# Prompt attention by pairs of heads: scores at two row places, a mask made by the scan, fp32 weights and values at two column places

## The chip, the cores and the metric

One NeuronCore of a Trainium2 chip runs the whole program in one launch. The metric is the device time in microseconds; the median of three runs stands for a kernel. The engines are named as in the profile: PE (TensorE), PEld (its weight loads), DVE (VectorE), ACT (ScalarE), POOL (GpSimd) and SP, whose queue issues all DMAs here.

## The reference

One step of a hybrid encoder layer, for a prompt of 1024 frames and for 8 decode sequences of 16 new frames with 1024 past ones. Width 1024, 16 heads of 64: group A (8 heads) has stick-breaking attention, group B (8 heads) has softmax attention over the own chunk of 64 frames and the 8 before it, with a learned bias.

```python
def stick_breaking(q, k, v, q_pos, k_pos):
    z = jnp.einsum('bqhd,bkhd->bhqk', q, k).astype(jnp.float32) * (HEAD_DIM ** -0.5)
    causal = k_pos[None, :] < q_pos[:, None]
    log_keep = jnp.where(causal, jax.nn.log_sigmoid(-z), 0.0)
    between = lax.cumsum(log_keep, axis=3, reverse=True) - log_keep
    w = jnp.where(causal, jnp.exp(jax.nn.log_sigmoid(z) + between), 0.0)
    return jnp.einsum('bhqk,bkhd->bqhd', w.astype(v.dtype), v)

def trunk_layer(x, p, ...):
    h = rmsnorm(x, g_mix)
    q_a, k_a, v_a, q_b, k_b, v_b = split_heads(h, w_in)
    a, o_b = stick_breaking(...), chunk_band_prompt(q_b, k_b, v_b, rel_table)
    mix = concat(rmsnorm(a), rmsnorm(o_b))           # per head
    x = x + mix @ w_out
    h = rmsnorm(x, g_ffn)
    x = x + (jax.nn.silu(h @ w_gate) * (h @ w_up)) @ w_down
    return x + sigmoid(rmsnorm(x, g_ple) @ w_ple_gate) * (p @ w_ple_proj)
```

All inputs and outputs are fp32.

## The kernel before

Most products are taken in three fp32r matmuls: both operands are split into a high part (rounded to fp32r) and a low part (the rest), and high x high, high x low and low x high are summed in PSUM (`mm3`, lines 105 to 108). The stages follow each other in this order and overlap at their borders.

1. *Projection* (`qkv`). Transposed, normed inputs stand in SBUF; weights come in column blocks of 256. It is a generator with 96 steps, each the matmuls of one output tile (24 of 256 or 384 columns). Queries and keys are written to DRAM transposed and split (`qkT`), values split in halves side by side (`vhl`).
2. *Decode of group A* beside the projection, up to some 333 us.
3. *Prompt attention* (`attention`). It is a generator too. A unit is one head and one tile `t` of 128 queries; there are 8 pairs of heads (the first 4 of group A), 16 heads, 128 units. One step of `run` does the scores of unit i, the flip of unit i-5 (`LAG`), the outputs of unit i-7 where `t` is odd, and the turn and finish of a head or pair that is through.
   - `head` loads, for one head, queries high and low on the two halves of the partitions, and the keys' high parts twice and low parts twice, so that two matmuls over 128 rows give all four partial products (lines 583 and 584). For group A a third matmul in bf16 adds -1e30 over the diagonal block (line 586). Scores have two PSUM banks (`s=2`).
   - Group A: ACT makes w = sigmoid(s) and keep = sigmoid(-s), DVE scans keep from the right (line 597), POOL multiplies w by the scanned keep (line 598). Group B: DVE adds the bias and takes the maximum (line 592), ACT takes the exponential (line 600).
   - `flip` transposes w by blocks of 128 x 128 on PE (line 616), four to a bank; ACT copies the bank rounded to fp32r into `wth` (line 620), DVE writes the rest into `wtl` (line 111, `sub`).
   - `outputs` multiplies values by weights, for two query tiles (256 columns) at once: the stationary operand holds the 64 high and the 64 low value columns of one head, so that two matmuls, with `wth` and `wtl`, make the sum's two halves on the two halves of the partitions (lines 639 and 640); ACT copies it out (line 643).
   - `turn` transposes the result back (line 654), DVE adds the halves (line 655); `finish` norms it and writes it to `mixp`.
   Transposes, outputs and turns share four PSUM banks (`t=4`), also with the transposes of the second decode (line 403) and of the embedding (line 842).
4. Beside attention run, one after the other: the last 30 projection steps, the *decode of group B* with the embedding product, and the mix with half of the output product. `advance(main, side, ratio)` interleaves two generators in program order. A planner orders each engine's instructions by its own costs, except where `manual_schedule` names engines: those keep the order of the program.
5. The other half of the output product, the feed-forward in seven products of blocks instead of eight (lines 1064 and 1327), the gate and the last norm.

## Time and profile before

| | |
|---|---|
| median of 3 runs | 1720.27 us (1717.31 to 1722.22) |
| span of the profiled execution | 1715.2 us; its own device time isn't listed, so it is read against the runs |
| busy share | PE 97%, PEld 83%, DVE 62%, ACT 47%, POOL 47% |
| chain that ended last | PE 81%, DVE 5%, DMA 5%, ACT 4% |
| moved by DMA | 293.48 MB |
| first score matmul, last flip | 333.4 us, 792.2 us |

The span runs from the first to the last instruction of the profiled execution; the time around it (start and end of the launch) is in the runs' times only. A row of the groups reads: line, engine, operation, output <- inputs by the program's names, shapes, count, then the busy time of the group in us and the mean duration of one in ns, then the idle time of the engine just before them and what ended it. Rows of the timeline begin with start and duration in us. Busy time counts a matmul to the end of its way through the array, so neighbouring matmuls overlap in it.

### The profile page before, as it was taken

How to read it: one execution, taken by the hardware profiler on the slowest of the kernel's cores; microseconds unless marked ns; L12 is line 12 of the kernel's file. 1: busy time of each engine (PE TensorE's matmuls, PEld its weight loads, DVE VectorE, ACT ScalarE, POOL GpSimd, SP SyncE). 2: the span in 40 equal slices, each digit the busy share in tenths (PEclk: the TensorE clock that was granted, in tenths of full speed). 3: DMA queues.
4: the chain of work that ended last, by engine and by line, in shares of the span. 5: the costliest groups of instructions: out<-in, count | busy, mean ns of one | idle time of the engine just before them, and what ended most of it. 6: DMA issues, size and time to landing. Idle time of an engine off the chain costs nothing.

```text
span 1715.2 us, 27832 instructions
## 1 busy us (share of the span) xinstructions
PE 1656.5 (97%) x10404; PEld 1421.2 (83%) x10404; DVE 1071.8 (62%) x1646; ACT 809.9 (47%) x1713; POOL 809.9 (47%) x590
## 2 busy tenths in 40 slices
PE   8999999999997999898989999999999999999998
PEld 7998888989996787787868888888888878888887
DVE  6111444367788766754787666655666587798875
ACT  5223545366677777643553333333333254433673
POOL 2313311277356512322355555555555379957763
PEclk9999999999999999999999999999999999999999
DMA  5846888666469895955423222222222597722222
GB/s 192 277 148 217 275 287 292 188 187 172 120 174 273 256 290 156 256 176 171 148 66 116 95 96 88 86 87 93 95 94 89 204 387 255 259 72 108 102 99 98
DMA packets 172808, 293.48 MB, mean 171 GB/s; under 512 B 16641, under 2 KB 96257, under 8 KB 170370
## 3 DMA queue, kind: packets, MB, share of 16 engines
q1 hardware_dynamic: 172674, 291.71, 52.0%
q8 instruction: 82, 1.34, 0.3%
q14 instruction: 52, 0.43, 0.1%
HBM read 204.77 MB, written 86.90 MB: 170 GB/s over the span
## 4 chain that ended last, share of the span: by engine, by line
PE 81%; DVE 5%; DMA 5%; ACT 4%; issue 2%; POOL 2%; SPq 0%; POOLq 0%; ACTq 0%; DVEq 0%
PE ps L1064 24%; PE ps L106 7%; PE ps L107 7%; PE ps L108 7%; PE pt L1327 4%; PE pt L1064 3%; PE ps L1327 3%; PE pt L616 3%; PE pt L403 3%; PE po L640 2%; PE po L639 2%; PE S L583 2%; PE acc L471 2%; PE sdec L426 1%; DMA v<-sv 1%
## 5 line engine op out<-in xcount | busy, mean ns | idle before, releaser
L111 POOL TENSOR_TENSOR wlo<-wraw,whi 128x512 fp32r<-128x512 f32 (+1 forms) x119 | 212.4, 1809 | 139.6 <-ACT whi L155 139.6
L106 PE MATMUL ps<-whi,hTh 128*128 128x256 f32 x576 | 168.5, 293 | 1.6 <-ACT st L263 1.6
L107 PE MATMUL ps<-wlo,hTh 128*128 128x256 f32 x576 | 165.2, 287 | 0.0
L108 PE MATMUL ps<-whi,hTl 128*128 128x256 f32 x576 | 164.9, 286 | 0.0
L597 DVE TENSOR_TENSOR_SCAN keep<-keep,zero 128x128 f32<-128x128 f32 (+4 forms) x64 | 102.1, 1604 | 32.6 <-ACT keep L589 32.2
L155 ACT CAST whi<-wraw 128x512 fp32r<-128x512 f32 (+1 forms) x122 | 88.6, 744 | 71.5 <-PE ps L1064 28.2
L598 POOL TENSOR_TENSOR w<-w,keep 128x127 f32<-128x127 f32 (+4 forms) x64 | 83.0, 1306 | 79.4 <-DVE keep L597 54.4
L106 PEld LDWEIGHTS ps<-whi,hTh 128*128 128x128 f32 x576 | 111.2, 193 | 7.5 <-issue 5.4
L107 PEld LDWEIGHTS ps<-wlo,hTh 128*128 128x128 f32 x576 | 111.3, 193 | 0.1
L108 PEld LDWEIGHTS ps<-whi,hTl 128*128 128x128 f32 x576 | 111.0, 193 | 0.5 <-DVE hTl L111 0.2
L111 DVE TENSOR_TENSOR wtl<-pt,wth 128x512 fp32r<-128x512 f32 (+1 forms) x192 | 94.4, 514 | 25.4 <-ACT wth L620 24.7
L620 ACT CAST wth<-pt 128x512 fp32r<-128x512 f32 (+1 forms) x192 | 85.1, 467 | 40.6 <-PE pt L616 40.1
L616 PE MATMUL pt<-ident,w 128*128 128x128 f32 x528 | 88.7, 280 | 6.6 <-DVE wtl L111 2.9
L639 PE MATMUL po<-wth,vk 128*128 128x256 f32 (+1 forms) x304 | 76.6, 283 | 0.4 <-DVE osb L655 0.4
L616 PEld LDWEIGHTS pt<-ident,w 128*128 128x128 f32 x528 | 62.3, 142 | 17.5 <-issue 5.0
L111 POOL TENSOR_TENSOR actl<-actr,acth 128x1024 fp32r<-128x1024 f32 (+1 forms) x22 | 61.5, 2795 | 32.4 <-DMA sr<-acts 20.7
L583 PE MATMUL S<-qk 128*128 128x384 f32 (+2 forms) x192 | 71.7, 375 | 5.0 <-ACT keep L589 3.1
L640 PE MATMUL po<-wtl,vk 128*128 128x256 f32 (+1 forms) x304 | 73.0, 283 | 0.0
L404 DVE COPY kT<-pt 128x512 f32<-128x512 f32 x48 | 33.0, 688 | 52.8 <-PE pt L403 48.8
L106 PE MATMUL ps<-hTh,whi 128*128 128x384 f32 x192 | 65.8, 343 | 0.0
L107 PE MATMUL ps<-hTl,whi 128*128 128x384 f32 x192 | 65.6, 342 | 0.0
L108 PE MATMUL ps<-hTh,wlo 128*128 128x384 f32 x192 | 65.2, 339 | 0.0
(446 smaller groups left out, 5276.9 us busy)
## 6 DMA issues: line engine op xcount, KB each, us to landing
draw<-in_cache_sb_k SPq DMA_DIRECT2D x32, 512.0 KB, 6.0
draw<-in_cache_sb_v SPq DMA_DIRECT2D x32, 512.0 KB, 6.0
act<-sg SPq DMA_DIRECT2D x11, 1152.0 KB
actr<-act SPq DMA_DIRECT2D x22, 576.0 KB, 5.4
wraw<-in_w_in SPq DMA_DIRECT2D x11, 1024.0 KB
wraw<-in_w_gate SPq DMA_DIRECT2D x11, 1024.0 KB, 5.6
wraw<-in_w_up SPq DMA_DIRECT2D x11, 1024.0 KB
v<-sv SPq DMA_DIRECT2D x36, 256.0 KB, 4.2
```

The costliest lines, as they stand in the source:

```text
L106: T.matmul(out, lhsT=ah, rhs=bh, start=start, stop=False)
L107: T.matmul(out, lhsT=ah, rhs=bl, start=False, stop=False)
L108: T.matmul(out, lhsT=al, rhs=bh, start=False, stop=stop)
L111: return eng.tensor_tensor(out, a, hi.bitcast(F32), op=ALU.subtract)
L155: A.copy(h[:, o], v[:, o])
L583: T.matmul(sc, lhsT=hd["qq"][:, qs], rhs=hd["kkh"][:, kc], start=True, stop=False)
L597: V.tensor_tensor_scan(rev, rev, zero[:, 0:1].to_broadcast([P, n]), 1.0, op0=ALU.mult, op1=ALU.add)
L616: T.transpose(pt[:, (c - c0) * P : (c - c0 + 1) * P], w[:, c * P : (c + 1) * P], ident)
L639: T.matmul(dst, lhsT=vs, rhs=wth[:, kb - base, c0:c1], start=(i == 0), stop=False)
L640: T.matmul(dst, lhsT=vs, rhs=wtl[:, kb - base, c0:c1], start=False, stop=(i == nkb - 1))
L1064: T.matmul(out, lhsT=a[x][:, k], rhs=b[y][:, k], start=(not more and k == 0 and n == 0), stop=(k == 3 and n == 2), skip_group_check=more)
L1327: T.matmul(out, lhsT=a[i][:, x, m * P : (m + 1) * P], rhs=b[j][:, x], start=(not more and x == 0 and n == 0), stop=(x == 1 and n == 2), sk ...
```

## The change

- A unit is a pair of heads and a query tile: 64 units. `LAG` is 2 units instead of 5; per step, the outputs of unit i-3 come first, then the scores of unit i, then the flip of unit i-2. The ratios of `advance` are halved or doubled accordingly. In the stretch beside the projection PE keeps the order of the program.
- Scores: three matmuls (high x high, high x low, low x high) for each of the two heads, on rows 0 to 63 and 64 to 127, alternately, into a bank for each head. Queries and keys are loaded once for the pair, in two halves of 512.
- The mask matmul goes. Group A's scan runs twice: over the diagonal block with the identity as second operand (`max`), which sets the running product to one at the diagonal and leaves zero beyond it, and then over the rest. A memset clears the last column of w.
- The weights are copied out of PSUM once, unsplit in fp32, by DVE and ACT in turn. Values are stored and loaded unsplit. `outputs` takes one fp32 matmul per head and key block, the two heads at columns 0 to 63 and 64 to 127.
- The result needs no addition of halves; it is turned back once for the pair.
- PSUM: `s=4, t=2`. Scores of group B are cut 256 columns from the end; the bias is loaded in two parts.

```diff
-LAG, RAWS, PT = 5, 7, 2
+LAG, RAWS, PT = 2, 7, 2
...
-    maskb = cst.tile([P, P], BF16, name="maskb")
...
-    vhl = [dram.tile([2, NT * P, 512], F32, name=f"v{g}") for g in range(2)]
+    vd = [dram.tile([2, NT * P, 256], F32, name=f"v{g}") for g in range(2)]
...
-                    for o in range(3):
-                        sv = stg.tile([P, 2, 384], F32R, name="sv", tag="sq").rearrange("p a b -> p (a b)")[:, :512]
-                        sv = sv.rearrange("p (h x d) -> p h x d", h=4, x=2)
-                        flat = st[:, o].rearrange("p (h d) -> p h d", d=HD)
-                        A.copy(sv[:, :, 0, :], flat)
-                        sub(G, sv[:, :, 1, :], flat, sv[:, :, 0, :])
-                        tok = slice((g * 3 + o) * P, (g * 3 + o + 1) * P)
-                        nc.sync.dma_start(vhl[grp][c, tok, :], sv.bitcast(F32).rearrange("p h x d -> p (h x d)"))
+                    rows = slice(g * 384, (g + 1) * 384)
+                    nc.sync.dma_start(vd[grp][c, rows, :].rearrange("(t p) n -> p t n", p=P), st)
...
+        def keys(pr, half):
+
+            grp, p_ = divmod(pr, 4)
+            cs = slice(half * 512, half * 512 + 512)
+            k = ap_.tile([P, 2, 512], F32R, name="k", tag=f"k{half}", bufs=2 - half)
+            for x in range(2):
+                nc.sync.dma_start(k[:, x].bitcast(F32), qkT[grp][1][x][p_][:, cs])
+            st[pr]["k", half] = k
+
+        def queries(pr, half):
+            grp, p_ = divmod(pr, 4)
+            cs = slice(half * 512, half * 512 + 512)
+            q = ap_.tile([P, 2, 512], F32R, name="q", tag=f"q{half}", bufs=1)
+            for x in range(2):
+                nc.sync.dma_start(q[:, x].bitcast(F32), qkT[grp][0][x][p_][:, cs])
+            st[pr]["q", half] = q
+
+        def values(pr, half):
+            grp, p_ = divmod(pr, 4)
+            v = ap_.tile([P, 4, P], F32, name="v", tag=f"v{half}", bufs=2 - half)
+            src = vd[grp][p_ // 2, half * 512 : half * 512 + 512, p_ % 2 * P : p_ % 2 * P + P]
+            nc.sync.dma_start(v, src.rearrange("(t p) n -> p t n", p=P))
+            st[pr]["v", half] = v
...
+            width = (7, 8, 6)[t % 3] * P
+            ws = [ap_.tile([P, width], F32, name="w", tag=f"w{t % 3}{hh}")[:, :n] for hh in range(2)]
+            keep = []
             if not grp:
+                for hh in range(2):
+                    turn[0] = (turn[0] + 1) % 3
+                    keep.append(ap_.tile([P, D], F32, name="keep", tag=f"keep{turn[0]}")[:, :n])
...
+            q = s_["q", t // 4][:, :, t % 4 * P : t % 4 * P + P]
+            lo = 0
+            while lo < n:
+                if grp:
+                    hi = n - 256 if n > 256 and lo == 0 else n
+                else:
+                    hi = n if lo else min(n, 512)
+                sc = [ps["s"].tile([P, 512], F32, name="S", tag="S")[:, : hi - lo] for hh in range(2)]
+                at = kb0 * P + lo
+                runs = []
+                while at < kb0 * P + hi:
+                    to = min(kb0 * P + hi, 512 if at < 512 else D)
+                    runs.append((at, to))
+                    at = to
+                for i, (at, to) in enumerate(runs):
+                    k = s_["k", at // 512][:, :, at % 512 : at % 512 + to - at]
+                    for n_, (x, y) in enumerate(((0, 0), (0, 1), (1, 0))):
+                        for hh in range(2):
+                            hs = slice(hh * 64, hh * 64 + 64)
+                            T.matmul(sc[hh][:, at - kb0 * P - lo : to - kb0 * P - lo], lhsT=q[hs, x], rhs=k[hs, y],
+                                     start=i == 0 and n_ == 0, stop=i == len(runs) - 1 and n_ == 2,
+                                     skip_group_check=len(runs) > 1)
+                for hh in range(2):
+                    w = ws[hh][:, lo:hi]
+                    if not grp:
+                        A.activation(w, sc[hh], AF.Sigmoid)
+                        A.activation(keep[hh][:, lo:hi], sc[hh], AF.Sigmoid, scale=-1.0)
...
+                    kp, d = keep[hh], n - P
+                    rev = kp[:, d:][:, ::-1]
+                    V.tensor_tensor_scan(rev, rev, ident[:, ::-1], 0.0, op0=ALU.mult, op1=ALU.max)
+                    if d:
+                        rev = kp[:, :d][:, ::-1]
+                        V.tensor_tensor_scan(rev, rev, zero[:, 0:1].to_broadcast([P, d]), kp[:, d : d + 1], op0=ALU.mult,
+                                             op1=ALU.max)
+                    G.memset(w[:, n - 1 :], 0.0)
+                    kept.append(G.tensor_tensor(w[:, : n - 1], w[:, : n - 1], kp[:, 1:], op=ALU.mult))
...
-                A.copy(wth[:, ks, qs], pv)
-                sub(V, wtl[:, ks, qs], pv, wth[:, ks, qs])
...
+            for hh, w in enumerate(ws):
+                for c0 in range(0, nb, 4):
+                    c1 = min(c0 + 4, nb)
+                    pt = ps["t"].tile([P, 512], F32, name="pt", tag="T")
+                    for c in range(c0, c1):
+                        T.transpose(pt[:, (c - c0) * P : (c - c0 + 1) * P], w[:, c * P : (c + 1) * P], ident)
+                    pv = pt[:, : (c1 - c0) * P].rearrange("p (k n) -> p k n", n=P)
+                    ks = slice(kb0 + c0 - base, kb0 + c1 - base)
+                    turn[1] = 1 - turn[1]
+                    (V.tensor_copy if turn[1] else A.copy)(s_["wt"][hh][:, ks, t % 2 * P : t % 2 * P + P], pv)
+            return s_["wt"]
...
-                vs = st[hh]["v"][:, kb].rearrange("p a d -> p (a d)")
-                dst = po[:, c0:c1]
-                T.matmul(dst, lhsT=vs, rhs=wth[:, kb - base, c0:c1], start=(i == 0), stop=False)
-                T.matmul(dst, lhsT=vs, rhs=wtl[:, kb - base, c0:c1], start=False, stop=(i == nkb - 1))
+                for hh in range(2):
+                    hs = slice(hh * 64, hh * 64 + 64)
+                    T.matmul(po[hs, c0:c1], lhsT=s_["v", kb // 4][:, kb % 4, hs], rhs=wt[hh][:, kb - base, c0:c1],
+                             start=i == 0, stop=i == len(order) - 1)
...
+        def turned(pr):
+
+            s_ = st[pr]
+            osb = s_["osb"] = ap_.tile([P, NP, P], F32, name="osb", tag="osb", bufs=1)
+            s_["ss"] = ap_.tile([P, NP, 2], F32, name="sso", tag="sso", bufs=2)
             for g in range(2):
                 pt = ps["t"].tile([P, 512], F32, name="pt", tag="T")
                 for t in range(4):
+                    T.transpose(pt[:, t * P : (t + 1) * P], s_["ob"][:, (g * 4 + t) * P : (g * 4 + t + 1) * P], ident)
+                (A.copy, V.tensor_copy)[g](osb[:, g * 4 : g * 4 + 4], pt.rearrange("p (t n) -> p t n", t=4))
+            A.activation(s_["ob"], osb.rearrange("p t n -> p (t n)"), AF.Square)
+            V.tensor_reduce(s_["ss"], s_["ob"].rearrange("p (t h d) -> p t h d", t=NP, h=2), axis=AX.X, op=ALU.add)
...
+            units = [(pr, t) for pr in prs for t in range(NP)]
             ws, wts = {}, {}
+            for i in range(len(units) + lag + 3):
+                m = i - lag - 1
+                if 0 <= m < len(units) and units[m][1] % 2:
+                    outputs(units[m][0], units[m][1] // 2, wts.pop(m))
                 if i < len(units):
+                    pr, t = units[i]
+                    if t == 0:
+                        keys(pr, 1)
+                        queries(pr, 1)
+                    elif t == 2:
+                        values(pr, 0)
+                    elif t == 3:
+                        values(pr, 1)
+                    elif t == 4 and pr < 7:
+                        prepare(pr + 1)
+                    ws[i] = scores(pr, t)
                 j = i - lag
                 if 0 <= j < len(units):
+                    pr, t = units[j]
+                    wts[j] = flip(pr, t, ws.pop(j))
+                if 0 <= m - 1 < len(units) and units[m - 1][1] == NP - 1:
+                    turned(units[m - 1][0])
+                    finish(units[m - 1][0])
...
-    banks(left, "left", s=2, t=4)
+    banks(left, "left", s=4, t=2)
     at = pool(left, "at", "left")
     run, pairs, done = attention(at, ps, LAG)
     att = run(range(8))
-    advance(project, att, 1.95)
+    with tc.manual_schedule(engines={mybir.EngineType.PE}):
+        advance(project, att, 0.98)
...
-    advance(att, dec, 0, 3)
+    advance(att, dec, 0, 2)
     beside = along(dec, embed(), 1.2, -3.0)
-    advance(att, beside, 1.0, 40)
+    advance(att, beside, 2.0, 20)
...
-    advance(att, side, 1.0)
+    advance(att, side, 2.0)
```

224 lines of the change are left out of this document (71 added, 153 removed).

## The prediction

> **What bounds the kernel now.** I read the page's shares and its chain of waits first, then a table of five stretches from the first score matmul to the end of the feed-forward's entry, then the groups of instructions by line, then single stretches of the timeline for the price of one matmul.
>
> ```profile
> span 1715.2 us, 27832 instructions
> PE 1656.5 (97%) x10404; PEld 1421.2 (83%) x10404; DVE 1071.8 (62%) x1646; ACT 809.9 (47%) x1713; POOL 809.9 (47%) x590
> PE 81%; DVE 5%; DMA 5%; ACT 4%; issue 2%; POOL 2%; SPq 0%; POOLq 0%; ACTq 0%; DVEq 0%
> ...
> core 0: us, PE busy (x) PEld busy (x) DVE busy (x) ACT busy (x) POOL busy (x), PEclk, DMA share, GB/s
> 333.00:500.00 167.00, 163.86 (x1194) 154.29 (x1193) 119.00 (x143) 111.19 (x275) 103.64 (x75) 0.99 0.57 164
> 500.00:575.00 75.00, 63.50 (x492) 53.65 (x491) 62.11 (x100) 58.49 (x144) 43.28 (x42) 0.95 0.87 253
> 575.00:725.00 150.00, 140.03 (x1199) 116.44 (x1198) 102.94 (x326) 109.34 (x293) 39.20 (x44) 0.98 0.81 240
> 725.00:800.00 75.00, 74.75 (x433) 64.66 (x431) 37.62 (x95) 30.32 (x70) 16.57 (x11) 1.00 0.54 173
> ```
>
> TensorE is the bound: 97% busy and 81% of the chain. The changed code runs from 333 to 800 us, beside the last 30 projection steps (to about 500), the second decode and the embedding product (to about 725), and the mix and half of the output product (to 800). In the first and last of these stretches TensorE has hardly a gap (163.86 of 167, 74.75 of 75). Only 500 to 575 is different: PE idles 11.5 us while DVE is busy 83% and ACT 78%. So a change here is worth what it takes off TensorE, plus what lighter ACT and DVE give back of the 11.5 us, less any new wait of TensorE. The work to be changed:
>
> ```profile
> L616 PE MATMUL pt<-ident,w 128*128 128x128 f32 x528 | 88.7, 280 | 6.6 <-DVE wtl L111 2.9 <-DVE kT L404 1.1 <-ACT w L600 0.9
> L639 PE MATMUL po<-wth,vk 128*128 128x256 f32 (+1 forms) x304 | 76.6, 283 | 0.4 <-DVE osb L655 0.4
> L583 PE MATMUL S<-qk 128*128 128x384 f32 (+2 forms) x192 | 71.7, 375 | 5.0 <-ACT keep L589 3.1 <-DVE mxp L592 1.7
> L426 PE MATMUL sdec<-kT,qbd 128*32 128x256 f32 (+1 forms) x384 | 31.9, 400 | 2.1 <-ACT keep L589 2.1
> L111 DVE TENSOR_TENSOR wtl<-pt,wth 128x512 fp32r<-128x512 f32 (+1 forms) x192 | 94.4, 514 | 25.4 <-ACT wth L620 24.7
> L620 ACT CAST wth<-pt 128x512 fp32r<-128x512 f32 (+1 forms) x192 | 85.1, 467 | 40.6 <-PE pt L616 40.1
> L404 DVE COPY kT<-pt 128x512 f32<-128x512 f32 x48 | 33.0, 688 | 52.8 <-PE pt L403 48.8
> ...
> L588 ACT ACTIVATE w<-S 128x512 f32<-128x512 f32 x40 | 24.7, 616 | 14.6 <-PE S L584 12.1 <-PE S L586 2.4
> L598 POOL TENSOR_TENSOR w<-w,keep 128x1023 f32<-128x1023 f32 x8 | 16.2, 2026 | 10.9 <-DVE keep L597 10.9
> L597 DVE TENSOR_TENSOR_SCAN keep<-keep,zero x64: 415/1624/3503, 337.5 to 557.2; 128x128 f32<-128x128 f32 x8, 128x256 f32<-128x256 f32 x8, 128x384 f32<-128x384 f32 x8, 128x512 f32<-128x512 f32 x8
> ```
>
> (In the last row: shortest, median and longest scan, in ns.) A matmul's mean there is its latency, and matmuls overlap; the price of one is the distance from its start to the next start. These rows (start, duration) give it:
>
> ```profile
> 519.82 0.22 PE L639 MATMUL po<-wth,vk 128*128 128x128 f32 x1
> 519.88 0.27 PE L640 MATMUL po<-wtl,vk 128*128 128x128 f32 x1
> ...
> 520.27 0.39 PE L584 MATMUL S<-qk 128*128 128x512 f32 x1
> 520.51 0.60 PE L616 MATMUL pt<-ident,w 128*128 128x128 f32 x4
> ...
> 521.42 0.23 PE L586 MATMUL S<-maskb,identb 128*128 128x128 bf16 x1
> 521.48 0.28 PE L616 MATMUL pt<-ident,w 128*128 128x128 f32 x1
> ...
> 423.62 0.33 PE L106 MATMUL ps<-hTh,whi 128*128 128x384 f32 x1
> 423.79 0.33 PE L107 MATMUL ps<-hTl,whi 128*128 128x384 f32 x1
> ...
> 181.94 0.38 PE L412 MATMUL pt<-ident,wdec 128*128 128x128 f32 x2
> 182.25 0.64 PE L426 MATMUL sdec<-kT,qbd 128*32 128x256 f32 x8
> 182.71 0.40 PE L471 MATMUL acc<-nv,wt 128*32 128x128 f32 x8
> 182.93 0.62 PE L471 MATMUL acc<-draw,wt 128*32 128x128 f32 x16
> 183.48 0.39 PE L106 MATMUL ps<-whi,hTh 128*128 128x256 f32 x1
> 183.70 0.28 PE L107 MATMUL ps<-wlo,hTh 128*128 128x256 f32 x1
> 183.82 0.29 PE L108 MATMUL ps<-whi,hTl 128*128 128x256 f32 x1
> ```
>
> An fp32r matmul costs 0.06 us for 128 columns, 0.12 for 256 (183.70 to 183.82), 0.17 for 384 and 0.23 for 512 (0.24 here before a change of kind); the bf16 mask matmul 0.06. The decode's own matmuls already run in fp32 at four column places. The program has 192 at line 426 (8 sequences, 6 chunks, 4 places) and the trace 384, so one fp32 matmul is two records. Eight records of 256 columns take 0.46 us and eight of 128 take 0.22: a round over all places costs 0.23 or 0.11, so the places run at the same time. Coming into that form costs 0.09 (0.31 for two transposes of 0.11), leaving it 0.11 (0.55 for four rounds), and the first full matmul after it 0.10 (0.22 for 0.12).
>
> **The change, part by part.** *Scores.* Before, with two matmuls per piece of keys and the mask: group A per head 128, 256, 384, 512, 384+256, 512+256, 512+384, 512+512 columns is 2.08 us, twice, plus eight masks (0.48) is 4.64; group B 0.58 and four of 0.29 is 1.74, twice, 3.48. Times eight heads: 37.1 + 27.8 = 64.9 us. After, three products for both heads, each on 64 rows. If the two row places overlap as the column places do, a piece costs three single matmuls: group A 2.08 x 3 = 6.24 per pair; group B, cut more finely (two more pieces from width 384, and at the border of the key halves), 1.78 x 3 = 5.34. Times four pairs each: 46.4 us, a saving of 18.5. No row of before shows row places. The nearest are the column places; without any overlap it is 92.8 us, a loss of 27.9. I take the overlap. The Trainium skill ("TensorE: Matmul & The Clock Gate", Part 3, measured speedup) has four row places reach 3.07 times instead of four; as an estimate, two places at that efficiency (0.77) would make 60 us of the 46.4, so the scores would save 5 us, not 18.5. The column rounds here, at 0.11 us for a two-pass matmul of 128, show no such loss, so I stay with them.
>
> *Outputs.* Before: 304 pairs of matmuls, 224 of 256 columns and 80 of 128: 2 x (224 x 0.12 + 80 x 0.06) = 63.4 us. After, 112 and 40 pairs of heads, each two rounds at two places: 112 x 0.44 + 40 x 0.22 = 58.1. Saving 5.3. One that does not overlap doubles it (+53); four places overlap in the rows above, so that end gets no chance of its own.
>
> *Turns.* 128 transposes become 64: 64 x 0.11 = 7.0 us saved. The 528 transposes of the weights stay. TensorE's own work: -18.5 - 5.3 - 7.0 = -31.
>
> *Changes of array form.* A step now goes full - (outputs) - scores - full: 32 entries into outputs, 64 into scores, 64 exits, 160 x 0.10 = 16, and the first matmul after an exit: 64 x 0.10 at most, half of them reach a transpose; I take 5. +21 us. Ends: +6 if only the column form costs (64 changes), +40 if the planner of the later stretches cuts each score burst in two. The Trainium skill ("TensorEngine Tiling (Array Packing)", Key Properties) says that a change of tiling mode drains the array; the 0.09 to 0.11 us rows agree for columns, and no run yet shows rows. By that sentence alone the row changes would cost too, as I count them.
>
> *The banks.* Scores get four PSUM banks instead of two, transposes and outputs two instead of four. Before:
>
> ```profile
> 523.15 0.63 PE L616 MATMUL pt<-ident,w 128*128 128x128 f32 x4 [1.38 <-DVE wtl L111]
> 523.89 0.61 ACT L620 CAST wth<-pt 128x512 fp32r<-128x512 f32 x1
> 524.21 0.68 DVE L111 TENSOR_TENSOR wtl<-pt,wth 128x512 fp32r<-128x512 f32 x1
> 524.81 2.28 DVE L597 TENSOR_TENSOR_SCAN keep<-keep,zero 128x1024 f32<-128x1024 f32 x1
> 524.94 0.44 PE L616 MATMUL pt<-ident,w 128*128 128x128 f32 x2 [0.92 <-DVE wtl L111]
> PE S L583 <- ACT keep L589: 3.1, 3, 1.6
> PE pt L910 <- DMA mixn<-mixp: 7.0, 2, 4.5
> ```
>
> A bank is held from 523.15 to 524.89. With one copy (0.69, line 404) 0.11 after the last transpose ends it is 1.48 us to the next transpose. A flip of a unit with more than four key blocks now fills four banks in a row: two go at once (0.44 + 0.27 on average), the third waits 1.48 - 0.71 = 0.75 us with DVE free, 3 us behind a scan of 2.28. Beside the projection, where PE's order is written out and nothing can step in, are 29 of 64 units: some 14 such flips and 4 turns, 18 x 0.75 = 13.5; the wait for the score banks (3.1, by the row) goes: +10. Behind the waiting transposes stand the next projection matmuls, so it all counts. Ends: 0 and +47 (18 at 1.9 us, 21 later ones at 0.75, less 3). I take the unqueued wait, since ACT loses 42 us of casts (half of 85.1) and DVE 47 of subtractions (half of 94.4; a copy costs what a subtraction does), besides what the turn and the value split took. Later the planner can put decode or output matmuls into the wait: 0.
>
> *Lag and chain.* Two pair steps instead of five head steps. A unit of 1024 keys needs eight sigmoids of 0.62, then scans of 2 x 2.28 and two short ones of 0.42 at the least, of which the first head's lie beside the last sigmoids, then a product of 2.03: some 10 to 13 us; beside the projection the two steps after it take about 17. Hidden there; for the three last group A units, without the projection, it is some 9 us, inside the stretch of 11.5 idle us. The 56 extra scans (0.42 us or more, 24 us of DVE at the least) and 64 memsets lie on engines that are 71% and 62% busy up to 500: nothing on the path. *Relief.* In 500 to 575 I take half of the 11.5 us; after it 10.0 us of idle, 7.0 of them waits for a DMA (last row), with, by the tiles' shapes, 8 MB of query and key loads, 4 of values and 5 of value writes fewer to move: 5. Together -11; ends 0 and -21. The queues of SP: half the loads, in halves of the keys, each one to four steps ahead of use: nothing. The value split, its 36 DMA writes and the decode's addition lie beside a full PE: nothing.
>
> Sum: -31 + 21 + 10 - 11 = -11 us. The profiled span is 1715.2 us, so 1704; the runs' median, 1720.27, is 5.1 above the span, so 1709.
>
> **Rivals.** *The transposes' banks decide* (slower). Place: third and fourth bank of a flip, PE's written order. For it: the scans of up to 2.28 us in front of a DVE copy, and DVE gets every 512-column piece of the large flips. Against it: ACT and DVE lose over 40 us each. It outweighs the rest from 21 + 3 us of waits, that is 1.3 us in each of the 18 places; at its upper end 1720 - 31 + 21 + 47 - 11 = 1746. *The row places do not overlap*: 1709 + 46 = 1755. For it: nothing in this trace runs so. Against it: the column places. *Overlap in part, or the gain given back in changes of form*: twice the bursts (+19 over my 21) or 14 us more for the scores: 1723, no change. That case is what the skill's 3.07 would make of it; the trace's column rounds speak against it. *All relief, cheap changes*: 6 for changes, no bank waits, 21 of relief: 1720 - 31 + 6 - 21 = 1674.
>
> **The numbers.** Forecast 0.44 (own range 1697 to 1722, three quarters of it below 1715), banks 0.18, no overlap 0.09, no change 0.13, all relief 0.16. The runs lie within 5 us, so 0.3% is what can be told. Faster 0.34 + 0.16 = 0.50; same 0.09 + 0.08 = 0.17; slower 0.33. The range reaches to 1676 and 1748, which leaves out about half of the last case and most of the one without overlap.
>
> **What would show it.** Score matmuls of 64 rows starting in twos almost at once, at 0.23 us per two of 512: right; 0.23 between the two: no overlap. The sum of the gaps at entries and exits near 0.1 each. PE's waits for the flip's copies beside the projection: about 14 us; over 25 us the forecast falls. The stretch from the first score to the end of the projection (167 us): about the same length, since there 29/32 of group A's savings (11 us of scores, 3 of outputs, 3 of turns) meet 29/64 of the 21 us and the 10 of the banks; what is gained lies after 500. More than 5 us of PE waiting for the products of group A at the flips would mean the lag is too short.

## The result and the profile after

The changed kernel takes 1771.86 us (median of four runs, 1768.07 to 1773.4) against 1718.79 for the kernel before (1714.85 to 1722.22): 1.0306 times as long, 95% interval 1.0283 to 1.033. Forecast were 1709, with a range from 1676 to 1748. The profiled execution spans 1771.6 us, against 1715.2. Ratios leave out two executions that took far longer than the others of their kernel (3250.26 us in the last experiment, 2332.22 of the kernel before beside it).

Page of the changed kernel: span, busy time of each engine, shares of the chain of waits, and the rows of the groups that answer to those shown of before.

```profile
span 1771.6 us, 27815 instructions
PE 1687.4 (95%) x10588; PEld 1393.9 (79%) x10588; DVE 1056.8 (60%) x1606; ACT 747.2 (42%) x1550; POOL 771.5 (44%) x611
PE 79%; DVE 6%; ACT 5%; issue 4%; POOL 3%; DMA 2%; SPq 0%; POOLq 0%; ACTq 0%; DVEq 0%
...
L641 PE MATMUL pt<-ident,w 128*128 128x128 f32 x528 | 87.7, 287 | 28.8 <-DVE wt L645 19.7
...
L645 DVE COPY wt<-pt 128x512 f32<-128x512 f32 (+2 forms) x96 | 59.4, 618 | 83.1 <-PE pt L641 82.5
```

ACT, DVE and POOL all got lighter, as the change says, and TensorE has fallen from 97% to 95% busy. But its busy time grew as well, from 1656.5 to 1687.4 us: of the 56.4 us that the span is longer, 30.9 are busy time of TensorE and 25.5 idle time. The transposes' idle time was 6.6 us in the old row (line 616) and is 28.8 here.

The same comparison by stage: the columns are start:end, length, busy time of PE, PEld, DVE, ACT and POOL with counts, granted TensorE clock, DMA share and GB/s. The borders are events that both kernels have: first score, last projection matmul, last embedding matmul, last matmul of the second half of the output product, end. First the kernel before, then the one after.

```profile
333.50:511.40 177.90, 174.76 (x1268) 164.53 (x1267) 129.25 (x155) 120.32 (x297) 108.50 (x80) 0.99 0.59 170
511.40:682.40 171.00, 157.74 (x1377) 128.96 (x1376) 123.06 (x320) 127.34 (x334) 63.51 (x70) 0.98 0.81 241
682.40:870.50 188.10, 172.82 (x966) 145.83 (x965) 119.08 (x277) 99.73 (x231) 59.31 (x47) 0.96 0.58 183
870.50:1715.20 844.70, 829.32 (x3748) 684.68 (x3746) 586.86 (x718) 325.61 (x532) 500.22 (x309) 1.00 0.36 130
```

```profile
327.50:543.50 216.00, 193.21 (x1398) 164.94 (x1398) 138.26 (x166) 101.14 (x244) 90.56 (x120) 0.95 0.32 105
543.50:727.50 184.00, 167.54 (x1399) 114.02 (x1398) 104.72 (x282) 100.44 (x269) 63.51 (x83) 0.96 0.62 202
727.50:923.90 196.40, 183.55 (x1075) 142.12 (x1074) 111.50 (x265) 90.37 (x205) 52.87 (x35) 0.97 0.46 155
923.90:1771.60 847.70, 829.47 (x3748) 684.56 (x3746) 589.06 (x718) 324.61 (x532) 500.77 (x309) 1.00 0.36 129
```

The first stage, beside the projection, is 38 us longer, the second 13, the third 8; the rest 3. (The first score comes 6 us earlier, because 80 projection matmuls, 9.5 us, that the kernel before ran ahead of it now lie behind it: of the 38 some 29 are new.) Over the first three stages PE's idle time (length less busy time) is 52.1 us where it was 31.7. The granted clock is lower in the first two stages (0.95 and 0.96 for 0.99 and 0.98).

PE's waits in the first stage, first of the kernel before, then of the one after (who waited, for what: us in total, times, longest):

```profile
PE S L583 <- ACT keep L589: 2.4, 2, 1.6
PE pt L616 <- POOL w L598: 0.5, 1, 0.5
```

```profile
PE pt L641 <- DVE wt L645: 13.3, 13, 3.6
PE pt L641 <- ACT wt L645: 3.5, 6, 1.2
PE S L597 <- DMA q<-qT0h: 3.4, 1, 3.4
PE pt L676 <- ACT wt L645: 2.6, 3, 0.9
PE po L662 <- ACT wt L645: 1.3, 1, 1.3
PE pt L641 <- POOL w L622: 1.1, 2, 0.5
PE pt L676 <- DVE wt L645: 0.9, 3, 0.3
```

Waits for the flip's copies are 21.6 us (13.3, 3.5, 2.6, 1.3, 0.9) where there were none. The timeline of PE, DVE and ACT after one step's scores, in the changed kernel, shows why a copy of ACT is late (three dots stand for rows left out):

```profile
401.77 0.66 PE L641 MATMUL pt<-ident,w 128*128 128x128 f32 x4
401.87 0.60 ACT L603 ACTIVATE w<-S 128x512 f32<-128x512 f32 x1 [0.52 <-PE S L597]
402.24 0.42 DVE L645 COPY wt<-pt 128x256 f32<-128x256 f32 x1 [0.88 <-PE pt L641]
402.37 0.59 ACT L604 ACTIVATE keep<-S 128x512 f32<-128x512 f32 x1
402.72 0.66 PE L676 MATMUL pt<-ident,ob 128*128 128x128 f32 x4 [0.30 <-DVE wt L645]
402.85 0.60 ACT L603 ACTIVATE w<-S 128x512 f32<-128x512 f32 x1
...
403.32 0.62 ACT L604 ACTIVATE keep<-S 128x512 f32<-128x512 f32 x1
...
403.80 0.40 ACT L645 COPY wt<-pt 128x256 f32<-128x256 f32 x1
404.05 0.64 ACT L677 COPY osb<-pt 128x512 f32<-128x512 f32 x1
404.26 0.33 PE L676 MATMUL pt<-ident,ob 128*128 128x128 f32 x1 [0.88 <-ACT wt L645]
```

Four transposes go out for the two heads (two each). DVE copies its bank at once; ACT's copy, for the other bank, starts at 403.80, behind the four sigmoids of the scores that PE issued ahead of the flip. Until it has run, the second bank is not free for the rest of the turn, and PE waits. ACT is 42% busy over the span and 47% in this stage (101.14 of 216); what counts is what stands ahead of the copy in its queue.

Most of the waits (14.2 of 21.6 us) are for copies of DVE. The longest one of this stage, 3.63 us:

```profile
369.33 0.63 PE L641 MATMUL pt<-ident,w 128*128 128x128 f32 x4 [0.66 <-DVE wt L645]
...
370.32 4.78 POOL L107 TENSOR_TENSOR wlo<-wraw,whi 128x1024 fp32r<-128x1024 f32 x2
...
370.69 2.26 DVE L617 TENSOR_TENSOR_SCAN keep<-keep,ident 128x128 f32<-128x128 f32 x1 [1.50 <-ACT keep L604]
...
372.86 0.66 DVE L645 COPY wt<-pt 128x512 f32<-128x512 f32 x1
...
373.58 0.69 PE L641 MATMUL pt<-ident,w 128*128 128x128 f32 x2 [3.63 <-DVE wt L645]
```

The bank is full at 369.96. In DVE's queue the new unit's scan stands ahead of the copy, and that scan waits for ACT's sigmoid until 370.69: DVE idles 1.50 us, 0.73 of them with the bank full. Then the scan takes 2.26 us, where most of its kind take 0.39 to 0.67. It is one of the scans that the change added; why it took so long is not shown, but POOL's subtraction (line 107) ran beside it.

In the third stage one new wait stands out. Before, then after, the largest row of each:

```profile
PE pt L910 <- DMA mixn<-mixp: 10.8, 3, 4.5
```

```profile
PE pt L922 <- POOL osb L695: 8.5, 1, 8.5
```

The waits for `mixn` have all but gone (0.5 us), but at the end of attention PE has nothing left but the last pair's result, which ACT, DVE and POOL are still norming.

### The profile page after: what moved, and what is told of

It reads as the page before. It is cut to its first block, busy times and chain, and to the rows that moved or that the text cites. A ratio compares the mean times of both kernels' runs of the same rounds, so it can differ in the third digit from the quotient of the medians.

```text
span 1771.6 us, 27815 instructions
## 1 busy us (share of the span) xinstructions
PE 1687.4 (95%) x10588; PEld 1393.9 (79%) x10588; DVE 1056.8 (60%) x1606; ACT 747.2 (42%) x1550; POOL 771.5 (44%) x611
## 4 chain that ended last, share of the span: by engine, by line
PE 79%; DVE 6%; ACT 5%; issue 4%; POOL 3%; DMA 2%; SPq 0%; POOLq 0%; ACTq 0%; DVEq 0%
PE ps L1076 24%; PE ps L102 7%; PE ps L104 7%; PE ps L103 7%; PE S L597 3%; PE po L662 3%; PE pt L1076 3%; PE pt L1339 3%; PE pt L641 3%; PE ps L1339 3%; PE pt L389 2%; PE acc L457 2%; PE sdec L412 1%; DMA q<-in_w_ple_gate 1%; PE pt L104 1%
## 5 line engine op out<-in xcount | busy, mean ns | idle before, releaser
L641 PE MATMUL pt<-ident,w 128*128 128x128 f32 x528 | 87.7, 287 | 28.8 <-DVE wt L645 19.7
L623 POOL TENSOR_TENSOR w<-w,keep 128x127 f32<-128x127 f32 (+7 forms) x64 | 81.2, 1272 | 76.9 <-DVE keep L620 67.2
L645 DVE COPY wt<-pt 128x512 f32<-128x512 f32 (+2 forms) x96 | 59.4, 618 | 83.1 <-PE pt L641 82.5
L597 PE MATMUL S<-k,q 64*128 64x256 f32 (+3 forms) x696 | 94.8, 335 | 4.0 <-DMA q<-qT0h 3.4
L620 DVE TENSOR_TENSOR_SCAN keep<-keep,zero 128x128 f32<-128x128 f32 (+6 forms) x56 | 93.6, 1677 | 1.4
L597 PEld LDWEIGHTS S<-k,q 64*128 64x128 f32 x696 | 66.3, 188 | 31.2 <-issue 21.1
L662 PE MATMUL po<-wt,v 128*64 128x256 f32 (+1 forms) x608 | 67.6, 357 | 1.6 <-ACT wt L645 1.3
L645 ACT COPY wt<-pt 128x128 f32<-128x128 f32 (+3 forms) x96 | 37.2, 388 | 62.1 <-PE pt L641 61.9
```

The costliest lines, as they stand in the source:

```text
L597: T.matmul(sc[hh][:, at - kb0 * P - lo : to - kb0 * P - lo], lhsT=q[hs, x], rhs=k[hs, y], start=i == 0 and n_ == 0, stop=i == len(runs) - ...
L620: V.tensor_tensor_scan(rev, rev, zero[:, 0:1].to_broadcast([P, d]), kp[:, d : d + 1], op0=ALU.mult, op1=ALU.max)
L641: T.transpose(pt[:, (c - c0) * P : (c - c0 + 1) * P], w[:, c * P : (c + 1) * P], ident)
L645: (V.tensor_copy if turn[1] else A.copy)(s_["wt"][hh][:, ks, t % 2 * P : t % 2 * P + P], pv)
L662: T.matmul(po[hs, c0:c1], lhsT=s_["v", kb // 4][:, kb % 4, hs], rhs=wt[hh][:, kb - base, c0:c1], start=i == 0, stop=i == len(order) - 1)
```

## Experiments

Two theories. B: the slowdown is the PSUM banks (four score banks, two for transposes and outputs), through PE's waits. F: it is the changes of array form and what goes with them. All ratios are to runs of the kernel before on the same chip; "stages" are the lengths of the first three stretches of the tables above (after: 216.0, 184.0, 196.4).

**Order beside the projection left to the planner**

```diff
-    with tc.manual_schedule(engines={mybir.EngineType.PE}):
-        advance(project, att, 0.98)
+    advance(project, att, 0.98)
```

> The changed kernel with one edit: beside the projection the planner orders PE again, instead of the program. The changed kernel takes 1771.9 us; from its first score to its last projection matmul it takes 216 us, 178 before the change. Theory B (two transpose banks, under an order in which nothing can step in): the planner puts projection matmuls into the waits, so PE's waits there fall from some 26 us to under 10 and the stretch to 190 to 200; time 1750 to 1758. Theory F (changes of array form): the planner cuts the bursts, the changes in that stretch rise from 67 to over 100 and cost 7 us more or so; time 1775 to 1785.

1777.77 us, 1.034 (1.0318 to 1.0363); stages 171.1, 230.8, 195.8. The first stage is free of waits, but the planner carried attention less far in it (150 transposes of weights, where the changed kernel does 222), and the second stage pays 47 us. The work was put off, not helped: this run does not separate the theories.

**Three score banks and three for the transposes; and two and four, as before**

```diff
-    banks(left, "left", s=4, t=2)
+    banks(left, "left", s=3, t=3)        # the other run: s=2, t=4
```

> The changed kernel with three PSUM banks for scores and three for transposes and outputs, instead of four and two. Theory B: PE's waits for the copies of the flips (26 us beside the projection) fall by two thirds, some wait for score banks comes up; the stretch of 216 us goes to about 198, and the later stretches gain 5; time about 1750. Theory F: no change beyond 5 us, 1767 to 1777. Theory L (lag of two units too short, the products of group A late): no change either, as the wait would only move from the bank to the product.

> The changed kernel with the banks as they were before: two for scores, four for transposes and outputs. Theory B: the flips' waits vanish (26 us beside the projection), but each piece of scores now takes both banks, so the next piece waits for four sigmoids of up to 0.62 us: 18 second pieces beside the projection at 2 us make 30 us or more; time 1770 to 1785. Theory F: no change beyond 5 us.

Three and three: 1754.93 us, 1.0206 (1.0185 to 1.0227); stages 206.3, 182.6, 189.2. Two and four: 1775.0 us, 1.0336 (1.0296 to 1.0376); first stage 221.0. PE's waits for banks and copies in the first stage, three and three first, then two and four:

```profile
PE S L597 <- ACT keep L604: 13.1, 12, 1.6
PE pt L641 <- DVE wt L645: 2.3, 5, 1.4
PE po L662 <- DVE wt L645: 1.6, 1, 1.6
```

```profile
PE S L597 <- ACT keep L604: 21.8, 24, 1.7
```

The wait goes from the transposes to the scores: a pair's unit of over 512 keys wants four score banks, and its flip four more, and there are six. B is confirmed for 17 us, and shown not to be all. Part of it lies far from the flips: the wait of 8.5 us for the last pair's norm stands in every run here with four and two banks (6.8 to 9.2 us) and in none with three or four banks for the transposes.

**All of group A's flip copies on ACT**

```diff
-   (V.tensor_copy if turn[1] else A.copy)(...)
+   (V.tensor_copy if turn[1] and grp else A.copy)(...)
```

> The changed kernel, with all copies of group A's flips on ACT (group B's still in turn). Theory B with the copies behind DVE's scans as the cause: the waits for DVE's copies beside the projection (15 us of flips, some more of turns) nearly vanish and those for ACT's grow by 3 to 5; the stretch of 216 us goes to about 203; time 1755 to 1760. If the number of banks alone is what counts, wherever the copy runs: ACT's copies wait behind sigmoids instead, no change beyond 5 us.

1786.39 us, 1.0392 (1.0367 to 1.0417); first stage 228.7, waits of transposes for ACT's copies 21.8 us and of turns 5.5. It got worse: a copy on ACT has no scan ahead of it, but ACT's queue holds the sigmoids of the unit whose scores PE issued just before, as the timeline above shows.

**The flip of head 0 ahead of the scores, that of head 1 behind them; alone, and with three and three banks**

```diff
+   j = i - lag
+   if 0 <= j < len(units):
+       flip(*units[j], ws[j], (0,))
    if i < len(units):
        ...
        ws[i] = scores(pr, t)
-       wts[j] = flip(pr, t, ws.pop(j))
+       wts[j] = flip(pr, t, ws.pop(j), (1,))
```

> The changed kernel with the flip of a unit in two: the first head's transposes and copies stand ahead of the step's outputs and scores, the second head's behind them. Work, banks and changes of form are the same but for the place. Theory B (four transpose banks wanted in a row where there are two): at the second head's flip the first head's banks have had the time of the scores to be copied, so PE's waits for the flips' copies beside the projection (20 us, 26 with turns and outputs) fall to 10 or less, though an output bank now comes right behind two flip banks; the stretch of 216 us goes to 200 to 207; time 1757 to 1763. If the copies are late because DVE and ACT are busy, and not because four are wanted at once, the waits stay: 1768 to 1775.

> The split flip together with three score and three transpose banks. Theory B: both effects add in part: beside the projection some 10 us of waits for score banks and few for copies are left; that stretch 195 to 200 us; time 1742 to 1750. It stays above the kernel before the change (1720), since the 40 us of form changes are not touched.

Alone: 1763.54 us, 1.0272 (1.0255 to 1.0289); first stage 204.3, waits for DVE's copies 8.8 instead of 13.3. That fits the queue: half of the copies no longer stand behind the new unit's sigmoids and scans. With three and three: 1755.2 us, 1.0218 (1.0203 to 1.0234), no better than three and three alone (1754.93). With three and three the waits for copies are already down to 3.9 us in the first stage (2.3 and 1.6 above), so that the split finds little left to mend, and the waits for the score banks, which it does not touch, stay.

**Score products on all 128 rows**

```diff
-   for n_, (x, y) in enumerate(((0, 0), (0, 1), (1, 0))):
-       for hh in range(2):
-           T.matmul(sc[hh][...], lhsT=q[hs, x], rhs=k[hs, y], ...)
+   for hh, x, y, first, last in ((0, 0, 0, 1, 0), (0, 0, 1, 0, 1), (1, 1, 0, 1, 1)):
+       T.matmul(sc[hh][...], lhsT=q[:, x], rhs=k[:, y], ...)
```

> The changed kernel with each piece's six score matmuls on 64 rows replaced by three on all 128 rows (it leaves the heads' scores apart undone: each head gets products summed over both heads' rows, one of the heads a single one). Where two row places overlap fully, PE's work is the same; what goes is the change of array form into and out of the scores. Theory F: the form changes that touch rows (about 5.7 us beside the projection, 16 beside the second decode, 8 in the stage after it) vanish, time 1771 - 30 = 1740 to 1748. Theory B: most of the loss is the banks; the waits for copies stay at 26 us, and the time falls by less than 15, as what is saved at the changes comes back as waits: 1757 to 1768.

The heads' scores are not kept apart in this kernel; it measures time alone. 1743.08 us, 1.0147 (1.0132 to 1.0163); stages 205.8, 173.6, 189.1. Three full matmuls stand for six on 64 rows, the same time if the places overlap fully (one burst takes 1.42 us as twelve matmuls, from 422.15 to 423.57 below, and 1.35 as six here, from 417.55 to 418.90); without the rows' form the kernel is 28.8 us faster. Counted by the distances of the starts in the trace, the score matmuls take 61.3 us in the changed kernel and 46.1 here (forecast: 46.4), and what the form changes add falls by some 24 us. The two are more than the run shows, because waits take some of it back: PE's idle time in the three stages grew from 52.1 to 61.5 us. Where the 15 us went shows in PE's timeline of the changed kernel, in the second stage:

```profile
640.61 0.33 PE L597 MATMUL S<-k,q 64*128 64x128 f32 x2
640.87 0.66 PE L641 MATMUL pt<-ident,w 128*128 128x128 f32 x4
641.46 0.72 PE L597 MATMUL S<-k,q 64*128 64x128 f32 x8
642.11 0.33 PE L641 MATMUL pt<-ident,w 128*128 128x128 f32 x1
642.37 0.74 PE L597 MATMUL S<-k,q 64*128 64x256 f32 x5
643.03 0.31 PE L457 MATMUL acc<-nv,wt 128*32 128x128 f32 x3
...
643.59 0.62 PE L597 MATMUL S<-k,q 64*128 64x256 f32 x3
```

The planner cuts a burst into pieces of 2, 8, 5 and 3 matmuls, with others between. Each piece pays for going in and out. In the piece of five, three starts are 0.12 us apart (642.59, 642.71, 642.83), and so are the last two of the piece of three: their partners on the other rows are elsewhere, and nothing overlaps.

**The heads' row places in turn**

```diff
-   for n_, (x, y) in enumerate(((0, 0), (0, 1), (1, 0))):
-       for hh in range(2):
-           hs = slice(hh * 64, hh * 64 + 64)
+   for hh in range(2):
+       hs = slice(hh * 64, hh * 64 + 64)
+       for n_, (x, y) in enumerate(((0, 0), (0, 1), (1, 0))):
```

> The changed kernel with the three products of one head issued first and then those of the other, so that no two neighbouring matmuls but one pair per piece lie at different row places. If the overlap is what makes six matmuls cost three, the scores' work rises from about 61 to over 100 us of PE (two thirds of 46 us more): time 1795 to 1810, less where PE waits anyhow. If row places overlap whatever the order, since a matmul of the other place may overtake: no change.

1774.18 us, 1.0326 (1.0311 to 1.0341): no change, the second of the two outcomes named. The starts still come in twos, 10 ns apart (421.876 and 421.886), although three matmuls of head 0 were issued ahead of three of head 1. The burst's row in the timeline of this kernel, then that in the changed one:

```profile
421.88 1.52 PE L597 MATMUL S<-k,q 64*128 64x512 f32 x12
423.32 0.77 PE L641 MATMUL pt<-ident,w 128*128 128x128 f32 x5
```

```profile
422.15 1.49 PE L597 MATMUL S<-k,q 64*128 64x512 f32 x12
423.57 0.66 PE L641 MATMUL pt<-ident,w 128*128 128x128 f32 x4
```

So how the heads alternate within a burst does not matter; whether the partners stand in the same burst does.

**PE's order written out in the second and third stages too, with three and three banks**

```diff
+    written = ExitStack()
+    written.enter_context(tc.manual_schedule(engines={mybir.EngineType.PE}))
     next(dec)
     ...
     advance(att, side, 2.0)
+    written.close()
```

> Three score and three transpose banks as in the run with three of each (1755 us), and PE's order written out as in the program also beside the second decode and the mix, where the planner had cut the bursts. Theory F (form changes cost what the planner splits): entries into row places fall from 85 to about 37 in the two later stages, and their changes from 35 us to under 25; time 1743 to 1750. Theory B: with a written order the waits for banks come up there as well, 10 to 20 us, and eat it: 1755 to 1770.

1749.32 us, 1.0171 (1.0151 to 1.019), 5.6 less than three and three alone, whose interval it just touches. The bursts stay whole: PE's busy time in the three stages falls from 543.6 to 515.1 us, and the form changes of the two later ones, counted by start distances, fall from some 26 to 15 and from 9 to 4 us. But PE may step aside no more, and new waits take most of it back: its idle time grows from 34.4 to 58.2 us. The largest new wait is for the score banks of group B, which DVE empties (`mxp`), 14.3 us where three and three alone had none.

**Both causes out, one after the other**

None of these kernels keeps the heads apart; they measure time alone. Full rows with three and three banks; then full rows and outputs as one full-column product (no form but the decode's own), with four and two banks; then the same with three and three.

```diff
-   for hh in range(2):
-       hs = slice(hh * 64, hh * 64 + 64)
-       T.matmul(po[hs, c0:c1], lhsT=s_["v", kb // 4][:, kb % 4, hs], rhs=wt[hh][:, kb - base, c0:c1], ...)
+   T.matmul(po[:, c0:c1], lhsT=s_["v", kb // 4][:, kb % 4], rhs=wt[i % 2][:, kb - base, c0:c1], ...)
```

> Both edits at once: score matmuls on all rows (heads not kept apart, three matmuls per piece for six) and three banks each. If row changes (28 us) and banks (17 us) are separate costs, they add: 1771 - 28 - 17 = 1726, within 5. If they overlap (waits take what the changes leave), 1735 to 1743.

> Score matmuls on all rows as before, and the outputs on all columns too: for each key block one fp32 matmul of both heads' values with the weights of one head in turn, for two matmuls at two column places (heads not kept apart; the same rounds for PE). No form change is left but the second decode's. Theory F: against the run with full rows alone (1743) the column changes vanish, 24 in the stage beside the projection (2.2 us), 26 and 24 later (about 4 and 3 us): 1732 to 1738. If column places are free: 1743.

> Three score and three transpose banks and no array forms at all: scores on all 128 rows and outputs as one full-column product per key block, so the two heads are not kept apart in scores and outputs, the rest is whole. It holds the forecast's work term alone with what is left of the bank waits. Accounting theory: the bank swap gains on this kernel what it gained on full rows (28.8), 1732.5 - 28.8 = 1704, with waits of scores and transposes beside the projection near 15 us, so that work (-31) and waits (+15) make 1719 - 31 + 15 = 1703. Rival, the bank swap's gain on full rows came from column forms being hidden in the waits: it gains only the 17 of the first try, 1715, no faster than with column forms. Second rival, the work saving is smaller than 31 and hidden by the clock: over 1715.

| | four and two banks | three and three | banks |
|---|---|---|---|
| the changed kernel | 1771.86 | 1754.93 | 17 |
| full rows | 1743.08 | 1714.27 | 28.8 |
| full rows and columns | 1732.47 | 1704.07 | 28.4 |

Ratios of the four new ones: 1714.27 is 0.9975 (0.9964 to 0.9986), 1732.47 is 1.0073 (1.0054 to 1.0093), 1704.07 is 0.9915 (0.99 to 0.9931). The column form costs 10.6 and 10.2 us, on either banks. The rows cost 28.8 with four and two and 40.7 with three and three, so the two causes overlap: with the row form in place the better banks gain some 12 us less. The last run came out at its forecast, 1704. PE's waits of it, over the whole span, the two largest:

```profile
PE pt L639 <- DVE wt L643: 11.5, 11, 4.3
PE S L595 <- ACT keep L602: 10.1, 13, 1.7
```

21.6 us, where before had 6.0 for the same two causes (3.1 for the score banks, 2.9 for `wtl`). The work shows in its first three stages:

```profile
326.70:522.90 196.20, 178.54 (x1157) 166.66 (x1158) 140.40 (x166) 100.47 (x244) 94.74 (x120) 0.97 0.35 114
522.90:684.10 161.20, 147.01 (x1178) 111.59 (x1177) 105.41 (x283) 100.97 (x271) 61.99 (x80) 0.95 0.71 234
684.10:853.90 169.80, 160.69 (x886) 134.85 (x885) 110.30 (x265) 88.23 (x202) 54.82 (x40) 1.00 0.53 179
```

PE is busy for 486.2 us in them, against 505.3 before, and 9.5 us of the 486.2 are projection matmuls that stood ahead of the first score before: 28.6 us less, where 31 of work were forecast to go. Its idle time is 41.0 us against 31.7: 15.6 us more for the two causes above, some 6 less for others. These are measurements of parts, not versions to use. To keep the heads apart without row places, scores need the four products per head of before, 18.5 us more, and outputs the column places, 10: an estimate of 1733, not run, which would not beat the kernel before.

**The kernel before with the scan's mask alone**

```diff
-   T.matmul(sc[:, hi - lo - P :], lhsT=identb, rhs=maskb, start=False, stop=True)
...
-   rev = keep[:, ::-1]
-   V.tensor_tensor_scan(rev, rev, zero[...], 1.0, op0=ALU.mult, op1=ALU.add)
+   rev = keep[:, d:][:, ::-1]
+   V.tensor_tensor_scan(rev, rev, ident[:, ::-1], 0.0, op0=ALU.mult, op1=ALU.max)
+   ...
+   G.memset(w[:, n - 1 :], 0.0)
```

> The kernel before the change with one part of the change alone: no mask matmul, the scan in two parts with the identity over the diagonal block, and the memset. It takes 64 mask matmuls off PE (0.06 us each, 4 us) and puts 56 scans (0.42 us or more, 24 us) on DVE, which is 71% to 83% busy where group A runs. If PE alone counts: 1714 to 1717. If DVE's added time shows in the stretch without the projection (500 to 575 us): 1720 to 1726.

1718.44 us, 0.999 (0.9978 to 1.0002): no difference that can be told. On this kernel the second scan and the memset cost nothing measurable (in the changed one such a scan stands ahead of the copy in the longest wait of the first stage), and the eight mask matmuls per head gain nothing to speak of.

## Why the prediction was wrong

Two steps of the sum failed, the changes of form (+21) and the banks (+10), each by more than the whole gain of 11 us that was forecast. By the last table, against 1719.5: the kernel without forms and with three and three banks is 15.4 us faster; +28.4 for four and two banks; +10.6 for the column form; +28.8 for the row form: 1771.9. The last three are differences of runs, so the sum closes by itself; in the other order they are 17 for the banks and 50.9 for the two forms.

- *Scores, -18.5.* The step was right where the order is written and mis-sized where it is not. Twelve matmuls (six of 512 columns, six of 384) take 1.42 us from 422.15 to 423.57: 3 x 0.23 + 3 x 0.17 = 1.20, and 0.22 for its first weights and for coming out. That is full overlap, and the rival without it falls. But the sum took every burst to be as written. In the planner's stages partners are cut apart; by start distances the scores went from 65.4 to 61.3 us, a saving of some 4 instead of 18.5. The Trainium skill ("TensorE: Matmul & The Clock Gate", Part 3) gives 3.07 for four row places; two places in a whole burst lose nothing here, and what was lost had another cause.
- *Outputs -5.3 and turns -7.0.* With the full-row scores they make the 31 for which the last run shows 28.6 of busy time. About right as a sum, not measured one by one.
- *Changes of form, +21.* The term is mis-sized. Counted in the trace's order of matmuls there are some 113 entries into the rows (28, 50 and 35 in the three stages) where 64 were counted: the planner cuts, which the text had as its upper end of +40. And one burst costs about 0.35 us, where the sum had some 0.28: 0.09 ahead of the first score, 0.11 at its first weights, 0.09 on leaving and 0.06 on the first transpose after it, by the single starts of one burst. Form changes and the overlap that is lost in cut bursts cost 39.4 us together in the runs with four and two banks, and 50.9 with three and three. The Trainium skill ("TensorEngine Tiling (Array Packing)", Key Properties) says that a change of mode drains the array; the trace agrees, for rows (0.09 us on entry) as for columns, whose form costs 10.2 to 10.6 us in the runs.
- *The banks, +10.* This step failed with the form changes: 28.4 us (17 with the forms in place) for the split into four and two, and 15.6 of waits that three and three still leave. The wait was priced as unqueued, 0.75 us, because ACT and DVE lose over 40 us each. But these are shares of busy time, and the copies queue behind the sigmoids and scans that PE's new order puts ahead of them: in the longest wait, of 3.63 us, DVE idled for 0.73 behind a scan that was not ready and then ran that scan for 2.26. The later stages were put at 0, since the planner could step in; there the copies cost 10.4 us of waits in the second stage, and the last pair's norm 8.5 in the third. The text had the size as its end of +47, and its first rival is what happened in part, but that rival left the forms at 21 and kept the relief: 1746 instead of 1772. Both ends came true together, and the range had been built from one at a time. The Trainium skill ("TensorEngine Tiling (Array Packing)", PSUM Bottleneck) has it that the copies out of PSUM may become the bottleneck once tiling makes TensorE faster. Waits for these copies did come up (21.6 us in the first stage), but not by that road: the kernel with neither form and four and two banks has 20.6 us of them there.
- *The sign named for it* (over 25 us of waits and the forecast falls) did not show, at 21.6. It was set too high, and it looked at one stage alone. Beside the waits, stretches at half the clock grew from 24 to 44 us in the records of the three stages, which can be up to 10 us of time. What brings them on was not settled (last section).
- *Relief, -11.* It came, but not in this kernel, where the banks took it back. The waits for `mixn` fell from 10.8 to 0.5 us as meant, and the wait of 8.5 for the last pair's norm took their place. PE's idle time in the second stage went from 13.3 us (171.00 - 157.74) to 16.5 (184.00 - 167.54), with ACT and DVE lighter by 27 and 18 us; 10.4 of it are waits for the flip's copies. With three and three banks PE idles 8.5 us in the second stage and 8.5 in the third, 11.6 less than before in the two; how much of that is due to the lighter engines was not taken apart.
- *Lag.* Right: 1.7 us of waits for group A's product. The added scans, which the text had nowhere on the path, came onto it by standing ahead of DVE's copies. *Queues of SP:* one wait of 3.4 us for the first queries, which the text had at nothing.
- *Length of the first stage.* "About the same" was wrong by 29 us.

## What to carry to other kernels

Price a wait for a copy by what stands ahead of it in its engine's queue at that moment; ACT, 47% busy in the first stage, held a full PSUM bank for 1.8 us here, and DVE, 64% busy, held one for 3.6, and when a unit's results are doubled the banks that it fills at once double too, so count first how many there are. A gain by array tiling is only had where the bursts stay whole: look at who orders the matmuls, count the entries and exits as they will be issued, and take both ends of two such costs together into the range if one change brings both.

## What the runs showed of the hardware

- Two row places of 64 in fp32r overlap fully (0.23 us for two matmuls of 512 columns), and the order of issue within a burst does not matter: three of one place ahead of three of the other still start in twos, 10 ns apart.
- Going into row form and out again costs about 0.35 us a burst, with the slower first matmuls on both sides.
- The granted clock of the first stage is 0.95 in the changed kernel, with 21.6 us of waits for copies, 1.00 where the planner kept PE busy, and 0.99 with three and three banks, which still has 17.0 us of waits for banks and copies; with two and four, whose waits are 21.8 us and none over 1.7, it is 0.95. Idle time alone does not set it: PE idles 17.5 us in the first stage with three and three (clock 0.99) and 17.7 with neither form and three and three (0.97). What does, these runs don't show.
- The scan of a diagonal block (128x128) took 0.39 to 0.67 us in 46 of its 56 cases in the changed kernel and 1.4 to 2.3 in ten. In all ten POOL worked for over 80% of the scan's time; but so it did beside some that took 0.42, and what the ten had in common was not taken apart.
